# Wider joins, a moved chain of forget gates, a tile for the bonus factors and another estimate in a trunk layer

## The chip, the core and the metric

The kernel runs on one core of one Trainium2 chip. The metric is the device time of one launch in microseconds (us), as the median of several runs; lower is better. The core's engines are PE (TensorE: matmuls, with its weight loads shown as PEld), DVE (VectorE), ACT (ScalarE), POOL (GpSimd) and SP (SyncE, which here only starts DMAs). Each engine works off its own list of instructions in order and waits on semaphores for what the others make.

## The reference

One layer on 512 tokens and 16 meta tokens put ahead of them (T = 528), width 1024. A projection of the normed input feeds a recurrent branch (RWKV7, 8 heads of 64), an attention branch with forget gates (FoX, 8 heads of 64) and two gates; their outputs are projected, gated, added, projected again, and an MLP follows.

```python
u = rmsnorm(h, norm_mix); proj = u @ w_in
y_rw = rwkv7_branch(proj[..., :C_RW], ...)      # recurrence S = S(diag(w) + a^T b) + v^T k, y = S r
#   ... y = groupnorm(y);  bonus = sum(r * k * r_k) * v;  out = (y + bonus) * g
y_fx = fox_branch(proj[..., C_RW:C_RW + C_FX], ...)
#   ... log_f = log_sigmoid(fl + b_f);  F = cumsum(log_f);  logits = q.k * scale + F_q - F_k
gates = sigmoid(proj[..., C_RW + C_FX:] + b_gate)
h = h + (gates_A * (y_rw @ w_out_rw) + gates_B * (y_fx @ w_out_fx)) @ w_o
h = h + square(relu(rmsnorm(h) @ w_up)) @ w_down
```

## The kernel before

**The first half, the mixer.** Features stand on partitions, tokens along the free dimension. Each weight matrix comes in blocks of 128 output features. A block is loaded by SP (`wraw`), rounded by ACT into `whi` (L548), its rest taken by DVE as `wlo` (L549), and multiplied in three passes (`projections`, L579: `whi` by `uhi`, `whi` by `ulo`, `wlo` by `uhi`). There are 24 such blocks of features in two parts of 264 tokens (some with one part of 512), and 16 of gates with 512 tokens. Their rows are named `pj`. Around them run two branches:

- The recurrence works on pairs of heads, 128 partitions each, in groups of two pairs (`recurrent`). For a pair, `decay` makes the decays (a scan `lc`, L882), `keys` norms the keys (`sq`, `pkk`, L894 to L913), POOL makes one product of the keys (`BK`, L912), `rows` makes the left factors `L` (L919 to L923) and a POOL product `sq` for the bonus (L924), `scores` multiplies chunk by chunk (`psr`, L948, and transposes `pbt`, L955), and `bonus` multiplies by `rkb`, a block of ones scaled by the bonus factors (L928, `pbn` L931). `rkb` shares the buffer "yT" with the tile `yT` of the group norm (L1160 to L1163) and with `tmp` of the inverse.
- For each group `inverse` inverts 18 triangular 64x64 matrices: first the 16x16 blocks by a long chain on DVE (L985, L986, transposes, `Dn` at L997), then joins by small matmuls (`pw`): L1011 makes a product of 64 matmuls of 32x32, DVE masks it to `W2` (L1012), L1017 and L1020 (64 each) multiply `W2` with the inverses of the 32x32 blocks, in one column order and in the other. Then L1033 and L1040 (32 each) join 32x32 blocks to 64x64. `W2` is zero but for the lower left 16x16 of each 32x32 block, and of the first result (`p1`, added to `Dn`) only the blocks of the even quarters of the partitions are read behind it.
- `chain` then runs the recurrence over nine chunks (`pch`: L1093, L1099, L1121, each of which waits for the one before through a DVE copy), and `group_norm` closes it.
- The attention takes pairs of heads as well: `fox_features` norms queries and keys (`pssq`, L674) and transposes values; `attention` makes scores (`psc`, L740), softmax on DVE and ACT, transposes (`ppt`, L777) and the product with the values (`py`, L791, L794). It needs the running sum `F` of the log forget gates: `forget` (L620 to L630) makes it of a row tile `f0` of 8 partitions by two ACT and four DVE operations, a scan among them (L629), stores it to DRAM, and each pair loads it back, spread over the partitions (`nF`, L728).

**What sets the order.** The branches are streams (generators). `Turns.run` lets the stream of the best rank go on whose inputs are ready by an estimate (`Clock`): every instruction is booked with a cost from `RATE` (a fixed part and one per element), and PE's order in the first half is the order in which the streams issue. Where no branch is ready, `pj` matmuls are taken: they are the filling between dependent steps. PE's order is thus fixed when the program is built; DVE, ACT, POOL and SP are ordered by the scheduler of the framework, `after` adding a few edges. In `recurrent`, `forget()` is called behind the `scores` of the first pair.

**The second half** (from L1251 on) multiplies by the output weights, norms, and runs the MLP with a Strassen-like scheme; there the matmuls follow each other nearly without a gap.

Of the kernel before, what the change touches and what calls it, by code (L numbers as in the profile page):

```python
# [9 lines left out]
F32 = mybir.dt.float32  # L10
# [9 lines left out]
T = 528  # L20
# [18 lines left out]
C_RK = 30  # L39
# [23 lines left out]
class Clock:  # L63
# [35 lines left out]
    def read(self):  # L99
# [3 lines left out]
        for x in new:  # L103
# [28 lines left out]
            else:  # L132
                size = max([cols(a) for a in outs + (ins if "Reduce" in str(x.opcode) else [])])
                if eng in self.RATE and "DMA" not in str(x.opcode):
                    fixed, per = self.RATE[eng]
                    end = self.book(eng, max(deps, self.last(out)), fixed + per * size) + fixed + per * size
                else:
                    cost = 0.3 + size * 128 * 4 / 2.0e5
                    end = self.book("DMA", max(deps, self.last(out)), cost) + cost + 2.0
# [48 lines left out]
def kernel(ctx, tc, ht, x, win, par, cst, gain, lora, wout, wo, wup, wdn, out, dbg=None):  # L188
# [97 lines left out]
    with ExitStack() as st:  # L286
# [32 lines left out]
        llo = up.tile([128, 2, T], F32R, name="llo")  # L319
        fF = kp.tile([8, T], F32, name="fF", tag="Bm", bufs=2)  # L320
        fF_d = dr.tile([8, T], F32, name="fF_d")
        f0 = kp.tile([8, T], F32, name="f0", tag="L0", bufs=2)
        f1 = kp.tile([8, T], F32, name="f1", tag="L1", bufs=2)
        lfs = [rp.tile([128, TP], F32, name=f"lf{i}", tag=("okk", "orr")[i]) for i in range(2)]
# [294 lines left out]

        def forget():  # L620

            s_ = act(f0, f0, AF.Identity, bias=pr[:8, C_BF:C_BF + 1])
            V.scalar_tensor_tensor(f1, f0, -1.0, f0, ALU.mult, ALU.max)
            pin = pinned(s_)
            after(act(f1, f1, AF.Exp, scale=-1.0), pin)
            after(act(f1, f1, AF.Ln, bias=1.0), pin)
            V.scalar_tensor_tensor(f1, f0, 0.0, f1, ALU.min, ALU.subtract)
            V.memset(f0, 1.0)
            V.tensor_tensor_scan(fF, f0, f1, 0.0, ALU.mult, ALU.subtract)  # L629
            nc.sync.dma_start(fF_d, fF)  # L630
            forgot.done = True

        class Fox:
# [33 lines left out]
            def normed(self, d, parts, gcol):  # L667
# [9 lines left out]
                c0 = parts[0][0]  # L677
                act(sq[:, c0:], sq[:, c0:], AF.Exp, scale=-0.5)
                V.scalar_tensor_tensor(f, f, gcol, sq[:, c0:], ALU.mult, ALU.mult)
                return f  # L680

        def fox_features():
# [4 lines left out]
            for p, x in enumerate(fox):  # L687
# [7 lines left out]
                k = yield from x.normed(x.dk, x.WHOLE, pr[:, C_KG:C_KG + 1])  # L695
                x.k_done.done = True
                yield x.v_in
                yield lambda: max(ck.ready(x.v), banks(2))
# [145 lines left out]
        class Pair:  # L844
# [70 lines left out]
            def rows(self):  # L915
# [7 lines left out]
                A.copy(l1[hss[1], :, 64:], l0[hss[1], :, 64:])  # L923
                G.tensor_tensor(self.sq[:, :S], self.orr[:, 64:], self.sg[:, 64:], ALU.mult)  # L924

            def bonus(self):
                rkb = rp.tile([128, 128], F32, name="rkb", tag="yT")
                after(V.tensor_scalar(rkb, ones_blk, self.col(C_RK), None, ALU.mult), last["DVE"])  # L928
                yield lambda: max(ck.ready(rkb, self.sq), banks(1))
                bp = psm("pbn")  # L930
                mm(bp, rkb, self.sq[:, :S], start=True, stop=True)  # L931
                self.bv = bv = rp.tile([128, S], F32, name="bv", bufs=2)
                V.tensor_tensor(bv, bp, self.ov[:, 64:], ALU.mult)
                act(bv, bv, AF.Identity, bias=self.col(C_LB))
# [25 lines left out]
        def inverse(g, Bms, late):  # L960
# [54 lines left out]
            for n, pr_, c in cells:  # L1015
                for q in range(4):
                    mm(p1[qs[q], n, :], Tt[qs[q], c, pr_, half(q)], W2[qs[q], n, :], start=True, stop=True)  # L1017
            for n, pr_, c in cells:
# [152 lines left out]
        def recurrent():  # L1171
# [4 lines left out]
            for g in range(2):  # L1176
                prs = pairs[2 * g:2 * g + 2]
                for j, q in enumerate(prs):
# [12 lines left out]
                    if g == 0 and j == 0:  # L1191
                        forget()
                    if j == 0:
# [406 lines left out]
```

## Time and profile before

| what | value |
|---|---|
| median of 3 runs | 837.0 us (835.97 to 838.46) |
| the profiled execution | 836.0 us |
| its span, first to last instruction | 834.2 us |
| PE busy in the span | 810.9 us (97%), 6014 matmuls, as many weight loads |
| DVE, ACT, POOL busy | 605.0, 452.7, 123.1 us |
| DMA | 95.90 MB in 51484 packets |

The span is what the views of the profile cover; 1.8 us of the profiled time lie around it. Of an instruction a row gives the start and the duration in us, then the engine, line, operation, result and operands, sizes, and in brackets the idle time of the engine ahead of it and what ended that. Matmuls overlap, so the distance of two starts says more of the rate than a duration does. A matmul of plain fp32 stands twice in the trace, one of fp32r and a transpose once; each has a weight load of its own.

### The profile page before, as it was taken

What the parts mean: (1) busy time and instruction counts of PE and PEld (TensorE: products, weight loads), DVE (VectorE), ACT (ScalarE), POOL (GpSimd) and SP (SyncE); (2) the same over time, 40 slices, a digit from 0 to 9 for tenths busy, and PEclk for the clock granted to TensorE, in tenths of its full rate; (3) what the DMA queues carried; (4) which work ended last, traced back from release to release, by engine and by line L of the source; (5) the groups of instructions that cost most, each with busy time, mean ns of one, the idle gap of its engine ahead of it and who ended that gap; (6) DMA issues with size and microseconds to landing.
All of it is one profiled execution on the core that took longest, in us unless ns stands there. A gap on an engine that the chain in (4) does not pass through costs nothing.

```text
span 834.2 us, 15768 instructions
## 1 busy us (share of the span) xinstructions
PE 810.9 (97%) x6014; PEld 666.4 (80%) x6014; DVE 605.0 (73%) x1197; ACT 452.7 (54%) x941; POOL 123.1 (15%) x123
## 2 busy tenths in 40 slices
PE   8989989999999899999999999999999999999998
PEld 6979877777868777677878889888888888888886
DVE  6797975596878836676356744975698679867988
ACT  7767537766666347764456623665345434543452
POOL 1031000010001000000022002100650074007400
PEclk9999999999999989999999999999999999999999
DMA  7231221221121402123587603632743274336532
GB/s 239 69 100 55 74 70 55 65 83 59 51 90 52 128 28 79 43 85 102 171 274 223 214 14 122 182 102 59 244 155 98 90 226 153 87 113 203 157 109 75
DMA packets 51484, 95.90 MB, mean 115 GB/s; under 512 B 5832, under 2 KB 7240, under 8 KB 51408
## 3 DMA queue, kind: packets, MB, share of 16 engines
q1 hardware_dynamic: 47680, 86.37, 32.8%
q0 software_dynamic: 1280, 4.20, 1.7%
q10 hardware_dynamic: 2448, 4.33, 1.5%
q8 instruction: 47, 0.77, 0.4%
q14 instruction: 29, 0.24, 0.1%
HBM read 88.56 MB, written 6.31 MB: 114 GB/s over the span
## 4 chain that ended last, share of the span: by engine, by line
PE 85%; DVE 7%; ACT 3%; issue 2%; DMA 2%; SPq 0%; DVEq 0%; ACTq 0%
PE pj L579 22%; PE po L1341 21%; PE po L1468 12%; PE pd L1468 5%; PE po L1251 4%; PE po L1313 3%; PE pj L394 1%; PE pd L1282 1%; PE po L1282 1%; PE psc L740 1%; PE py L794 1%; PE psr L948 1%; PE pssq L674 1%; DVE wlo L549 1%; PE ppt L777 1%
## 5 line engine op out<-in xcount | busy, mean ns | idle before, releaser
L579 PE MATMUL pj<-uhi,whi 128*128 128x264 f32 (+1 forms) x480 | 166.8, 347 | 0.0
L579 PE MATMUL pj<-uhi,wlo 128*128 128x264 f32 (+1 forms) x480 | 154.5, 322 | 2.5 <-DVE wlo L549 2.5
L579 PE MATMUL pj<-ulo,whi 128*128 128x264 f32 (+1 forms) x480 | 154.5, 322 | 0.0
L240 DVE TENSOR_TENSOR wlo<-wraw,whi 128x512 fp32r<-128x512 f32 x84 | 82.5, 993 | 33.5 <-ACT whi L240 33.5
L579 PEld LDWEIGHTS pj<-uhi,whi 128*128 128x128 f32 x480 | 91.0, 190 | 13.7 <-issue 5.3
L579 PEld LDWEIGHTS pj<-uhi,wlo 128*128 128x128 f32 x480 | 90.9, 189 | 9.8 <-DVE wlo L549 2.9
L579 PEld LDWEIGHTS pj<-ulo,whi 128*128 128x128 f32 x480 | 91.2, 190 | 6.6 <-issue 1.9
L1341 PE MATMUL po<-zlo,whi 128*128 128x512 f32 (+1 forms) x248 | 94.8, 382 | 0.0
L1341 PE MATMUL po<-zhi,whi 128*128 128x512 f32 (+1 forms) x248 | 94.8, 382 | 0.0
L1341 PE MATMUL po<-zhi,wlo 128*128 128x512 f32 (+1 forms) x248 | 94.8, 382 | 0.0
L240 ACT CAST whi<-wraw 128x512 fp32r<-128x512 f32 x84 | 51.2, 616 | 51.4 <-PE po L1341 17.0
L548 ACT CAST whi<-wraw 128x512 fp32r<-128x512 f32 x78 | 47.8, 617 | 43.4 <-PE pj L579 40.7
L549 DVE TENSOR_TENSOR wlo<-wraw,whi 128x512 fp32r<-128x512 f32 x78 | 53.8, 695 | 17.6 <-ACT whi L548 17.2
L1390 POOL TENSOR_TENSOR t<-traw 128x512 f32<-128x512 f32 x24 | 38.6, 1626 | 173.1 <-DMA traw<-in_wdn 120.9
L274 ACT CAST whi<-t 128x512 fp32r<-128x512 f32 x64 | 39.9, 623 | 44.5 <-DVE wlo L274 27.2
L1468 PE MATMUL po<-wlo,fhi 128*128 128x512 f32 (+1 forms) x164 | 63.4, 387 | 0.1
L1468 PE MATMUL po<-whi,flo 128*128 128x512 f32 (+1 forms) x164 | 62.8, 384 | 0.0
L1468 PE MATMUL po<-whi,fhi 128*128 128x512 f32 (+1 forms) x164 | 62.3, 384 | 0.0
L274 DVE TENSOR_TENSOR wlo<-t,whi 128x512 fp32r<-128x512 f32 x64 | 43.5, 689 | 24.3 <-ACT whi L274 24.0
L1357 ACT CAST fhi<-R 128x768 fp32r<-128x768 f32 (+1 forms) x32 | 30.2, 944 | 48.3 <-DVE R L1364 24.9
L1341 PEld LDWEIGHTS po<-zhi,wlo 128*128 128x128 f32 x248 | 46.6, 188 | 9.1
L1341 PEld LDWEIGHTS po<-zlo,whi 128*128 128x128 f32 x248 | 46.6, 188 | 9.1
(330 smaller groups left out, 1701.8 us busy)
## 6 DMA issues: line engine op xcount, KB each, us to landing
wraw<-in_win SPq DMA_DIRECT2D x84, 256.0 KB, 2.6
wraw<-in_wup SPq DMA_DIRECT2D x60, 256.0 KB, 3.1
wraw<-in_wdn SPq DMA_DIRECT2D x48, 256.0 KB, 2.7
traw<-in_wdn SPq DMA_DIRECT2D x48, 256.0 KB, 3.5
gd<-gt ACTq DMA_DIRECT2D x16, 256.0 KB, 2.2
wraw<-in_wout SPq DMA_DIRECT2D x16, 256.0 KB, 3.8
gl<-gd SPq DMA_DIRECT2D x16, 256.0 KB, 3.5
traw<-in_wdn POOLq DMA_DIRECT2D x16, 256.0 KB, 3.1
```

What stands on the lines that cost most here:

```text
L240: casts.append((A.copy(hi, raw), low.tensor_tensor(lo, raw, hi.bitcast(F32), ALU.subtract)))
L274: return A.copy(hi, x), V.tensor_tensor(lo, x, hi.bitcast(F32), ALU.subtract)
L548: after(A.copy(hi, raw), last["ACT"])
L549: after(V.tensor_tensor(lo, raw, hi.bitcast(F32), ALU.subtract), last["DVE"])
L579: mm(po, a, b[:, k, a0:a1], start=n == 0, stop=n == 23)
L1251: mm(po, a, ys[k][:, b, :], start=n == 0, stop=n == 11)
L1282: mm(pd[i], a[:, k, 128 * i:128 * i + 128], b, start=k == 0 and n == 0, stop=k == 7 and n == 2)
L1313: mm(po, a[:, k, 128 * i:128 * i + 128], b[:, k, :], start=n == 0, stop=n == 23)
L1341: mm(po[:, t0:t1], a, b[:, k, t0:t1], start=n == 0, stop=n == 23)
L1357: A.copy(fhi[:, j, a:b], R[:, a:b])
L1390: eng.tensor_tensor(t, sums[c, pair] if c in (T1, T2) else c, d, ALU.add)
L1468: mm(x[i][:, cols], a[:, k, left, 128 * rows:128 * rows + 128], c[:, cols], start=start and k == 0 and n == 0, stop=stop and k == n_pairs ...
```

## The change

Four things are changed.

1. In `inverse`, the first product with `W2` is made by 32 matmuls with 32 rows and 64 columns (L1026) in place of 64 of 32x32: those of the odd quarters are left out, whose results nothing reads, and the weights of the even ones are as wide as both quarters.
2. `forget` is split. `biased` (the ACT operation that adds the bias) stands where `forget` stood; the rest is issued by `fox_features` behind the keys' norm of the first pair, in tiles of the attention's pool (the buffers of `nF0`, `nF1` and `pT0`), and the memset of ones goes from DVE to POOL. `normed` now keeps its last ACT operation as `d["s"]`.
3. `rkb` has a buffer of its own and is made in `rows`.
4. `Clock` counts the part per element of a DVE operation twice if it is a scan, if its result has an innermost stride over 4 elements, or if it transposes from such a stride.

```diff
+                    if eng == "DVE" and (getattr(x, "is_tensor_tensor_scan", False) or any(a.ap[-1][0] > 4 for a in outs + (ins[:1] if "Transpose" in str(x.opcode) else []))):
+                        per *= 2
...
-        fF = kp.tile([8, T], F32, name="fF", tag="Bm", bufs=2)
-        f1 = kp.tile([8, T], F32, name="f1", tag="L1", bufs=2)
...
-        def forget():
-
-            s_ = act(f0, f0, AF.Identity, bias=pr[:8, C_BF:C_BF + 1])
-            V.scalar_tensor_tensor(f1, f0, -1.0, f0, ALU.mult, ALU.max)
-            pin = pinned(s_)
-            after(act(f1, f1, AF.Exp, scale=-1.0), pin)
-            after(act(f1, f1, AF.Ln, bias=1.0), pin)
-            V.scalar_tensor_tensor(f1, f0, 0.0, f1, ALU.min, ALU.subtract)
-            V.memset(f0, 1.0)
-            V.tensor_tensor_scan(fF, f0, f1, 0.0, ALU.mult, ALU.subtract)
+        forgets = [fp.tile([8, T], F32, name=f"forget{i}", tag=tag) for i, tag in enumerate(("nF0", "nF1", "pT0"))]
+        def biased():
+            return act(forgets[0], f0, AF.Identity, bias=pr[:8, C_BF:C_BF + 1])
+        def forget(prev):
+            fa, fb, fF = forgets
+            V.scalar_tensor_tensor(fb, fa, -1.0, fa, ALU.mult, ALU.max)
+            pin = pinned(prev)
+            after(act(fb, fb, AF.Exp, scale=-1.0), pin)
+            after(act(fb, fb, AF.Ln, bias=1.0), pin)
+            V.scalar_tensor_tensor(fb, fa, 0.0, fb, ALU.min, ALU.subtract)
+            G.memset(fa, 1.0)
+            V.tensor_tensor_scan(fF, fa, fb, 0.0, ALU.mult, ALU.subtract)
             nc.sync.dma_start(fF_d, fF)
...
-                act(sq[:, c0:], sq[:, c0:], AF.Exp, scale=-0.5)
+                d["s"] = act(sq[:, c0:], sq[:, c0:], AF.Exp, scale=-0.5)
...
                 x.k_done.done = True
+                if p == 0:
+                    forget(x.dk["s"])
...
+                self.rkb = rp.tile([128, 128], F32, name="rkb")
+                after(V.tensor_scalar(self.rkb, ones_blk, self.col(C_RK), None, ALU.mult), last["DVE"])
             def bonus(self):
-                rkb = rp.tile([128, 128], F32, name="rkb", tag="yT")
-                after(V.tensor_scalar(rkb, ones_blk, self.col(C_RK), None, ALU.mult), last["DVE"])
+                rkb = self.rkb
...
             for n, pr_, c in cells:
-                for q in range(4):
-                    mm(p1[qs[q], n, :], Tt[qs[q], c, pr_, half(q)], W2[qs[q], n, :], start=True, stop=True)
+                for e, hs in enumerate(hss):
+                    mm(p1[hs, n, :], Tt[qs[2 * e], c, pr_, :], W2[qs[2 * e], n, :], start=True, stop=True)
...
                     if g == 0 and j == 0:
-                        forget()
+                        biased()
```

What the scheduler makes of it is seen in the engines' orders. The first place is PE's at the joins of the first group; the row of the scores `psc` and the `pj` rows are filling there. Before:

```order
L740 MATMUL psc<-ka,qa 128x144 x2
L674 MATMUL pssq<-fsq,cs 128x512
L579 MATMUL pj<-uhi,whi 128x512
L579 MATMUL pj<-ulo,whi 128x512
L579 MATMUL pj<-uhi,wlo 128x512
L1017 MATMUL pw<-AX_1271,Tt 32x32 x64
L1020 MATMUL pw<-Tt,AX_1271 32x32 x64
```

In the changed kernel (its lines are 9 further down):

```order
L748 MATMUL psc<-ka,qa 128x144 x2
L579 MATMUL pj<-uhi,whi 128x512
L579 MATMUL pj<-ulo,whi 128x512
L579 MATMUL pj<-uhi,wlo 128x512
L1026 MATMUL pw<-AX_1271,Tt 64x32 x32
L1029 MATMUL pw<-Tt,AX_1271 32x32 x64
```

The 128 matmuls in a row have become 96, and the norm's matmul `pssq` now stands behind them. Ahead of L1020 (the old L1011) there are six `pj` of 512 tokens more than there were.

The second place is DVE's order in the first pair of the recurrence, from the keys' factor `KT` to the first `wlo` behind the left factors `L`; `f` are the tiles of the forget gates, `lw` small weights. Before:

```order
L910 SCALAR_TENSOR_TENSOR KT<-okk,lc 128x9x64
L623 SCALAR_TENSOR_TENSOR f_112<-f_111 8x528
L911 SCALAR_TENSOR_TENSOR BK<-tha,KT 128x9x64
L308 SCALAR_TENSOR_TENSOR orr<-pj,pr_65,tm 128x264
L913 TENSOR_TENSOR KT<-BK,P 128x1152
L922 TENSOR_TENSOR L_661<-orr,P 128x9x64
L838 TENSOR_TENSOR lw_1920<-lraw,lw_1919 128x128
L627 SCALAR_TENSOR_TENSOR f_112<-f_111,f_112 8x528
L549 TENSOR_TENSOR wlo<-wraw,whi 128x512
```

Now:

```order
L918 SCALAR_TENSOR_TENSOR KT<-okk,lc 128x9x64
L310 SCALAR_TENSOR_TENSOR orr<-pj,pr_65,tm 128x264
L846 TENSOR_TENSOR lw_1903<-lraw,lw_1902 128x128
L919 SCALAR_TENSOR_TENSOR BK<-tha,KT 128x9x64
L310 SCALAR_TENSOR_TENSOR orr<-pj,pr_65,tm 128x264
L921 TENSOR_TENSOR KT<-BK,P 128x1152
L930 TENSOR_TENSOR L_662<-orr,P 128x9x64
L549 TENSOR_TENSOR wlo<-wraw,whi 128x512 x2
```

Both operations on `f` have left this stretch, and the one small weight `lw` behind `L` as well.

The third place is where they went: DVE's order at the keys of the second pair, from `sg` (the factor of the keys) to the normed keys `okk`. Before:

```order
L904 TENSOR_TENSOR sg<-sg,okk 128x528
L304 MEMSET tm 128x1
L308 SCALAR_TENSOR_TENSOR orr<-pj,pr_65,tm 128x264
L899 TENSOR_SCALAR sq<-pkk 128x264
L549 TENSOR_TENSOR wlo<-wraw,whi 128x512
L899 TENSOR_SCALAR sq<-pkk 128x264
L308 SCALAR_TENSOR_TENSOR orr<-pj,pr_65,tm 128x264
L905 SCALAR_TENSOR_TENSOR okk<-okk,pr,sq 128x528
```

Now (the row L635 is the scan):

```order
L912 TENSOR_TENSOR sg<-sg,okk 128x528
L306 MEMSET tm 128x1
L310 SCALAR_TENSOR_TENSOR orr<-pj,pr_65,tm 128x264
L633 SCALAR_TENSOR_TENSOR forget_432<-forget_431,forget_432 8x528
L549 TENSOR_TENSOR wlo<-wraw,whi 128x512
L635 SCALAR_TENSOR_TENSOR forget_433<-forget_431,forget_432 8x528
L907 TENSOR_SCALAR sq<-pkk 128x264 x2
L549 TENSOR_TENSOR wlo<-wraw,whi 128x512
L310 SCALAR_TENSOR_TENSOR orr<-pj,pr_65,tm 128x264
L913 SCALAR_TENSOR_TENSOR okk<-okk,pr,sq 128x528
```

And POOL's order at the same time, where the memset that the scan waits for stands behind the product `BK` of this pair:

```order
L826 MEMSET sg 128x48
L826 MEMSET orr 128x48
L920 TENSOR_TENSOR BK<-sg,lc 128x9x64
L634 MEMSET forget_431 8x528
L932 TENSOR_TENSOR sq<-orr,sg 128x512
```

One operation on the forget gates and the scan now stand ahead of the two `sq`, of which the first pair's place had two and the memset. Between `okk` and the product `KT` behind it, two `wlo` stood before; they now stand elsewhere, with one evacuation of the values (`ov`) in their place. PE takes six `pj` of 264 tokens more ahead of this pair's `pkk`.

## The prediction

> **What bounds the kernel now.** I read the busy time by halves first, then PE's waits in the half that the change touches, then PE's timeline at each wait. The windows view gives start and end of a stretch, its length, busy time and instructions of PE, PEld, DVE, ACT and POOL, the granted clock, the DMA share and GB/s.
>
> ```profile
> 0.00:421.50 421.50, 402.27 (x4122) 325.47 (x4122) 299.80 (x772) 256.18 (x609) 24.68 (x51) 0.99 0.27 87
> 421.50:834.20 412.70, 408.66 (x1892) 340.95 (x1892) 305.24 (x427) 196.56 (x333) 98.40 (x72) 1.00 0.46 143
> ```
>
> PE sets the end in both halves: it is idle for 19.2 us of the first and 4.0 of the second. The change leaves the second half as it is, and of PE's own work it alters only the joins. So its worth must come from PE's idle time in the first half, and from what PE does at less than its pace. The waits view, for PE in 0 to 422 us, gives who waited for whom, the sum, the number and the longest:
>
> ```profile
> PE pw L1020 <- issue: 5.8, 2, 3.5
> PE pj L579 <- DVE wlo L549: 2.5, 1, 2.5
> PE pbn L931 <- DVE rkb L928: 1.8, 1, 1.8
> PE pw L1011 <- DVE AX L997: 1.8, 2, 0.9
> PE pch L1099 <- DVE Rs L1095: 1.7, 3, 0.7
> ```
>
> The four largest stand at places that the change edits. The largest waits for no engine ("issue"), so I looked at PE's timeline around both of its stops:
>
> ```profile
> 116.89 0.40 PE L579 MATMUL pj<-uhi,wlo 128*128 128x512 f32 x1
> 117.22 1.26 PE L1017 MATMUL pw<-AX,Tt 32*32 32x32 f32 x126
> 118.33 1.07 PE L1020 MATMUL pw<-Tt,AX 32*32 32x32 f32 x102
> 121.72 0.46 PE L1020 MATMUL pw<-Tt,AX 32*32 32x32 f32 x24 [2.32 <-issue]
> 122.70 0.63 PE L579 MATMUL pj<-ulo,whi 128*128 128x512 f32 x1
> 123.12 0.63 PE L579 MATMUL pj<-uhi,wlo 128*128 128x512 f32 x1
> 125.75 0.39 PE L579 MATMUL pj<-uhi,whi 128*128 128x512 f32 x1
> 125.98 0.39 PE L579 MATMUL pj<-ulo,whi 128*128 128x512 f32 x1
> 126.53 1.20 PE L1033 MATMUL pw<-AX,Bm 32*32 32x32 f32 x64
> ...
> 288.79 1.26 PE L1017 MATMUL pw<-AX,Tt 32*32 32x32 f32 x126
> 289.90 0.45 PE L1020 MATMUL pw<-Tt,AX 32*32 32x32 f32 x31
> 293.88 1.50 PE L1020 MATMUL pw<-Tt,AX 32*32 32x32 f32 x95 [3.52 <-issue]
> ```
>
> Each stop lies inside a burst of 256 short matmul records, which with their weight loads are 512 entries of PE's queue in some 2.2 us (117.22, and the next row 1.11 later for the first half of them). The page and the DMA view of the two stops (windows 119 to 121.72 and 290.3 to 293.88) show what moves:
>
> ```profile
> q8 instruction: 47, 0.77, 0.4%
> ...
> q8 instruction: 1, 0.02, 2.9%
> ...
> q8 instruction: 1, 0.02, 1.5%
> ```
>
> Over the run, 47 packets of 16 KB for 6014 matmuls and as many weight loads make 256 entries each; in each stop exactly one packet moves. I read both as PE having run through its fetched instructions faster than they come. Counted on PE's order, a boundary of 256 entries falls where each stop begins, 24 of L1020's 128 records before its end in the first and 95 in the second (102 + 24 and 31 + 95 stand above; two more each are mixed with L1017's). The boundary before it lies 128 records earlier, in L1017: about 118.1 and 289.1. From there to the resumption at 121.72 and 293.88 it is 3.6 and 4.8 us: that is the supply for one block, against which a burst is to be measured.
>
> The Trainium skill ("Runtime: NRT & Kernel Launch", section "Instruction fetch mechanics") says that instructions come in blocks of 16 KiB, 256 each, and that the cost of crossing a boundary is mostly hidden. The packets agree with the size; the two stops of 2.32 and 3.52 us speak against hidden here, and were the page right for bursts too, the stops would have another cause and survive: that is rival A, below.
>
> **The change part by part.** The sum is made against the profiled execution (836.0 us), then moved by the 1.0 us by which the median (837.0) stands above it.
>
> *The stops (1).* Now 64 + 128 records of L1026 and L1029 take the place of 128 + 128, with psc and three pj ahead of them. In the new order a boundary falls 32 records into L1029 in both inverses, and the one before it near the end of the preceding L1020 (the old L1011). From there to the need lie some 0.2 us of that burst, psc, pj (in the first inverse 115.02 to 117.22 held psc, pssq and three pj, of which pssq's 0.56 leaves), L1026, and 0.3 of L1029: 3.7 to 3.9 us. Against a supply of 3.6 to 4.8 that leaves a wait of 0 to 1.1 in each. I take 0.4 each: 5.8 goes to 0.8, **-5.0** (-5.8 to -3.6).
>
> *The half clock behind the stops (2).* The granted clock after each:
>
> ```profile
> 121.90:125.30 3.40, 3.40 (x32) 2.66 (x21) 1.41 (x2) 0.00 (x0) 0.00 (x0) 0.50 0.02 5
> 292.60:299.40 6.80, 5.52 (x105) 3.81 (x105) 2.61 (x8) 0.32 (x1) 0.00 (x0) 0.50 0.01 2
> ```
>
> Behind both long stops it is 0.50, for 3.4 and 6.8 us, of which PE worked 3.4 and 5.5. At that clock two pj start 0.42 us apart (122.70, 123.12), at full clock 0.23 (125.75, 125.98): 45% of the time is lost. That is 1.5 us in the first. In the second PE resumes at 293.88: 5.5 us, 2.5. Of these 4.0 I keep 3.3 as gained, since pauses of up to a microsecond may still lower the clock for a slice at one place: **-3.3** (-4.0 to 0).
>
> *The tile for rkb (3).*
>
> ```profile
> 242.99 0.28 DVE L928 TENSOR_SCALAR rkb<-cs,pr 128x128 f32<-128x128 f32 x1
> 243.42 1.10 PE L931 MATMUL pbn<-sq,rkb 128*128 128x512 f32 x2 [1.84 <-DVE rkb L928]
> ```
>
> rkb waited for the group norm's yT, whose buffer it shared. With its own tile it is made with the left factors, long before. Four of its instructions move, one per pair, 0.28 us each, into `rows`, where DVE's other work surrounds them. Its other operand, POOL's sq, is made with the left factors as well. **-1.8** (-1.8 to 0, if something else is late there).
>
> *The first pair (4).* PE's longest wait for an engine is here:
>
> ```profile
> 46.30 0.69 DVE L623 SCALAR_TENSOR_TENSOR f<-f 8x528 f32<-8x528 f32 x1
> ...
> 49.92 0.27 DVE L838 TENSOR_TENSOR lw<-lraw,lw 128x128 fp32r<-128x128 f32 x1
> 50.12 0.69 DVE L627 SCALAR_TENSOR_TENSOR f<-f,f 8x528 f32<-8x528 f32 x1
> 50.74 0.67 DVE L549 TENSOR_TENSOR wlo<-wraw,whi 128x512 fp32r<-128x512 f32 x1
> ...
> 51.47 0.50 PE L579 MATMUL pj<-uhi,wlo 128*128 128x512 f32 x1 [2.49 <-DVE wlo L549]
> ```
>
> Two operations on f, 0.62 us each from start to next start, and lw (0.20) leave the stretch ahead of this wlo, while PE's order up to it stays. 1.4 of the 2.49 us go, 1.1 remain: **-1.4** (-2.5 to -0.5). The lower gain stands if the wlo is held by its operand instead.
>
> *The first joins (5).* L1011 waits for AX 0.86 and 0.93 us (1.8 in two). Ahead of it there are six pj of 512 tokens more in the first inverse, 1.4 us at 0.23, behind the same chain on DVE. In the second PE has more filling too, but the softmax of two blocks now stands in DVE's chain. **-1.6** (-1.8 to 0).
>
> *L1026 itself (6).* Half the records, twice the rows and columns. The nearest row is L1033 at 126.53: 64 records, two of the four rows of tiles in use, 1.20 us, as long as 128 records of L1017 with four. So no PE time is gained: **0** (-0.9 to +0.2 for both inverses; half of 1.1 us each would go if a record's count decided).
>
> *The change of tile size (7).* From the pj at 116.89 to the first 32x32 matmul it is 0.33 us, against 0.23 between pj: 0.1 for a change of tile. One more per inverse: **+0.2**. The Trainium skill ("TensorEngine Tiling (Array Packing)", section "Key Properties") says that changing the mode drains the engine, which speaks against a second tile shape in the joins; the 0.33 agrees in kind, and the sum would be the same by the row.
>
> *The second pair (8),* where the forget gates went.
>
> ```profile
> 74.64 1.42 POOL L912 TENSOR_TENSOR BK<-sg,lc 128x576 f32<-128x576 f32 x1 [20.71 <-DVE tm L304]
> ...
> 235.79 0.49 POOL L965 MEMSET Ain<- 128x448 f32 x1 [8.27 <-PE pyt L1152]
> ...
> 55.21 1.24 DVE L629 TENSOR_TENSOR_SCAN fF<-f,f 8x528 f32<-8x528 f32 x1
> ...
> 82.49 0.68 DVE L549 TENSOR_TENSOR wlo<-wraw,whi 128x512 fp32r<-128x512 f32 x1
> 83.77 0.68 DVE L549 TENSOR_TENSOR wlo<-wraw,whi 128x512 fp32r<-128x512 f32 x1
> ...
> 85.77 0.55 PE L955 MATMUL pbt<-cs,KT 128*128 128x128 f32 x3 [0.29 <-DVE KT L913]
> ```
>
> Here the scan (1.24) and one operation on f (0.62) stand ahead of both sq, and behind the scan's operation L633 the ones of POOL: its memset starts behind BK, at 76.1, and by the nearest memset takes 0.5, so the scan starts near 76.6 at the earliest. While it waits, DVE's two sq, orr and okk are queued behind it, and PE's psr and pbt wait for these. By this sq ends some 1.5 us later. Against it two wlo (1.2 us) leave the way to KT and one ov (0.45) enters, and PE has six pj of 264 more (6 x 0.12 = 0.7) ahead. Net +0.3 on the 0.29 that stands there: **+0.3** (-0.5 to +1.5; the upper end is the 1.5 with no filling). The forget DMA, the load of nF and the memset of POOL are over by about 86 us, and the first scores come at 115: no wait.
>
> *The rest (9).* Doubling some costs in the estimate reshuffles the recurrence's chain and the attention behind it; the order shows about as many dense steps of `pch` as before. pch waits 1.7 us in 3 of its 52 steps, 0.57 each. I take two more such waits, **+1.0** (-2.0, these and the 0.3 of pbt gone, to +4.0, seven more).
>
> Sum: -5.0 - 3.3 - 1.8 - 1.4 - 1.6 + 0 + 0.2 + 0.3 + 1.0 = -11.6, so 824.4 in the profiled execution's frame and **825.4** as median.
>
> **The rivals.**
>
> *A: the stops stay.* They have a cause that fewer records do not remove, or the boundary costs its 2.3 and 3.5 us wherever it falls in a burst; L1029 is still 128 records long. Against it: the page counts 47 packets, and only the two in the longest bursts stop PE. Terms 1 and 2 come back: 825.4 + 8.3 = 833.7.
>
> *B: the stops shorten, the clock still halves* behind one or both. For it: the clock is a reaction to idle time, and 0.4 to 1.1 us may remain. The price is 1.5 to 3.3: 827 to 829.
>
> *C: the change does not do what it says.* DVE is busy 71% of the first half, so waits removed at rkb, at the joins and in the first pair form again behind other operations (+4.8), on top of A: 838.5, no difference to be measured.
>
> *D: slower.* The order on PE is fixed by the estimate. If the doubled costs lead it to place the recurrence's steps with less filling than DVE needs, PE waits at `pch` step after step, 0.57 us each. It decides from (837.0 + 2.5 - 825.4) / 0.57 = 25 more of the 52 steps; 28 give 841. Against it: three of 52 wait now, and the new order is no denser.
>
> **How the numbers follow.** Forecast 0.57 at 825.4, its own range 819 to 830 (a part of the bounds of 1, 2, 4 and 9 at once; all at their ends would be 818 to 839). B 0.17, A 0.12, C 0.08, D 0.06. About 0.3% (2.5 us) is what a measurement of this kernel can tell from no change. Faster: forecast, B and two thirds of A, 0.82; same: C and a third of A, 0.12; slower: D, 0.06. The range 818 to 834 leaves out C, D and a part of A and of the forecast's tails, about 0.2.
>
> **What would show it.** In the changed kernel's waits of PE, "issue" at the joins' lines should be under 1.5 us in sum (A: near 5.8), and no slice of clock 0.50 should stand near 120 and 295 us (B: one or two). The wait of pbn for rkb should be gone, that of pj for wlo near 51 us be about 1.1, that of L1020 for AX near nothing. pbt or psr of the second pair should wait under 1 us, pch under 4. The forecast is wrong if the queue's boundary falls elsewhere than counted, or if DVE's new order in the second pair or in the chain makes PE wait by more than the bounds of 8 and 9.

## The result, and the profile after

| | time, us (median) | its profiled execution | span | ratio to before, with its 95% interval |
|---|---|---|---|---|
| before | 837.15 | 836.0 | 834.2 | |
| changed | 827.47 (826.25 to 829.23) | 826.42 | 824.6 | 0.9886 (0.9859 to 0.9912) |

The change gains 1.1%, 9.7 us in the medians and 9.6 in the spans; forecast were 11.6. Of all executions behind the tables and ratios here, one, of a kernel among the last experiments, took 1130.28 us at a mean granted clock of 0.655 and is left out. The windows view of the changed kernel, cut where the second half begins (columns as before: length, busy time of PE, PEld, DVE, ACT, POOL, clock, DMA share, GB/s):

```profile
0.00:412.00 412.00, 399.83 (x3995) 326.34 (x3995) 301.30 (x771) 255.21 (x609) 22.78 (x52) 1.00 0.28 89
412.00:824.60 412.60, 408.67 (x1892) 341.04 (x1892) 305.19 (x426) 197.51 (x333) 97.87 (x72) 1.00 0.46 144
```

The second half lasts 412.6 us against 412.7, so all of the gain lies in the first, 421.5 to 412.0. Its idle time on PE fell from 19.2 to 12.2. PE's waits there:

```profile
PE pj L579 <- DVE wlo L549: 2.5, 1, 2.5
PE pbt L964 <- DVE KT L921: 2.1, 2, 1.3
PE pch L1108 <- DVE Rs L1104: 1.7, 3, 1.2
PE warm L403 <- DVE ones L328: 1.5, 1, 1.5
PE psc L748 <- DVE nm L759: 1.5, 1, 1.5
```

The rows for issue (5.8), for rkb (1.8) and for AX ahead of the first joins (1.8) are gone. The wait for wlo stands at 2.5 as before, pbt waits 2.1 in place of 0.3, and psc has a wait of 1.5 that is new. PE's timeline at the first joins:

```profile
118.25 0.40 PE L579 MATMUL pj<-uhi,wlo 128*128 128x512 f32 x1
118.58 2.05 PE L1026 MATMUL pw<-AX,Tt 32*64 32x32 f32 x64
120.56 1.29 PE L1029 MATMUL pw<-Tt,AX 32*32 32x32 f32 x128
121.78 0.50 PE L579 MATMUL pj<-uhi,whi 128*128 128x512 f32 x1
```

No stop is left in either product. The 64 records of L1026 take 1.98 us (118.58 to 120.56), where the 128 of the old L1017 took 1.1.

### The profile page after: what moved, and what is told of

It is laid out like the page before. It is cut to its first block, busy times and chain, and to the rows that moved or that the text cites. A ratio compares the mean times of both kernels' runs of the same rounds, so it can differ in the third digit from the quotient of the medians.

```text
span 824.6 us, 15506 instructions
## 1 busy us (share of the span) xinstructions
PE 808.5 (98%) x5886; PEld 667.4 (81%) x5886; DVE 606.5 (74%) x1196; ACT 452.7 (55%) x941; POOL 120.6 (15%) x124
## 4 chain that ended last, share of the span: by engine, by line
PE 86%; DVE 5%; ACT 5%; issue 2%; DMA 1%; SPq 0%; POOL 0%; DVEq 0%; ACTq 0%
PE pj L579 22%; PE po L1350 21%; PE po L1477 12%; PE po L1260 5%; PE pd L1477 5%; PE po L1322 3%; PE pj L394 1%; PE po L1291 1%; PE pd L1291 1%; PE psc L748 1%; PE py L802 1%; PE psr L957 1%; PE ppt L785 1%; PE pch L1108 1%; DVE wlo L549 1%
## 5 line engine op out<-in xcount | busy, mean ns | idle before, releaser
L579 PE MATMUL pj<-uhi,whi 128*128 128x264 f32 (+1 forms) x480 | 164.2, 342 | 0.0
L242 DVE TENSOR_TENSOR wlo<-wraw,whi 128x512 fp32r<-128x512 f32 x84 | 80.3, 966 | 35.5 <-ACT whi L242 35.5
L549 DVE TENSOR_TENSOR wlo<-wraw,whi 128x512 fp32r<-128x512 f32 x78 | 52.7, 685 | 23.7 <-ACT whi L548 23.0
L1350 PEld LDWEIGHTS po<-zhi,whi 128*128 128x128 f32 x248 | 46.6, 188 | 9.0
```

The source lines that it names most:

```text
L242: casts.append((A.copy(hi, raw), low.tensor_tensor(lo, raw, hi.bitcast(F32), ALU.subtract)))
L549: after(V.tensor_tensor(lo, raw, hi.bitcast(F32), ALU.subtract), last["DVE"])
L579: mm(po, a, b[:, k, a0:a1], start=n == 0, stop=n == 23)
L1350: mm(po[:, t0:t1], a, b[:, k, t0:t1], start=n == 0, stop=n == 23)
```

## The experiments

**Where the gain lies, and whether the stops are PE's own instructions.** Four kernels, measured together. The first is the changed kernel with the old joins, the third the kernel before with the new ones:

```diff
-                for e, hs in enumerate(hss):
-                    mm(p1[hs, n, :], Tt[qs[2 * e], c, pr_, :], W2[qs[2 * e], n, :], start=True, stop=True)
+                for q in range(4):
+                    mm(p1[qs[q], n, :], Tt[qs[q], c, pr_, half(q)], W2[qs[q], n, :], start=True, stop=True)
```

> The changed kernel with the first product with W2 again as 64 matmuls of 32x32 (the other three parts stay). Theory (PE runs out of fetched instructions in a burst of 512 queue entries): a boundary of 256 entries falls 31 records before the end of the second product in the first inverse and 97 before it in the second, each with 128 quick records ahead of it. PE stops there for issue, 2 to 3.7 us each, the clock halves behind at least one of them; L1026 takes 1.1 us in place of 2.0. Time 827.5 + 5.8 + 3.5 - 1.8 = 835.0 (833.5 to 836.5). Rival (the stops had another cause, which the other three parts removed): no stop for issue, L1026 shorter by 0.9 each, 825.7.

Measured: 836.25 us, ratio 0.998 (0.9964 to 0.9997). Without the joins almost nothing of the gain is left. PE's timeline at the two inverses:

```profile
120.08 0.42 PE L1026 MATMUL pw<-AX,Tt 32*32 32x32 f32 x28 [0.78 <-issue]
...
120.35 1.02 PE L1029 MATMUL pw<-Tt,AX 32*32 32x32 f32 x96
123.81 0.65 PE L1029 MATMUL pw<-Tt,AX 32*32 32x32 f32 x31 [2.43 <-issue]
...
292.31 0.99 PE L1026 MATMUL pw<-AX,Tt 32*32 32x32 f32 x95 [0.76 <-issue]
...
296.04 1.27 PE L1029 MATMUL pw<-Tt,AX 32*32 32x32 f32 x97 [2.46 <-issue]
```

The stops are back, 31 and 97 records before the end, as counted. The burst is now stopped twice, at both boundaries in it, 128 records apart.

> The kernel before with the wide joins alone. Theory: both stops for issue go (-5.8), no half clock near 120 and 295 us (-4.0), L1026 costs 0.9 more in each inverse (+1.8), the waits at rkb (1.8) and at the first product for AX (1.8) stay: 837.1 - 8.0 = 829.1 (827.5 to 831). Rival (the gain needs the other parts as well): 833 or more.

The edit is the reverse of the diff above, in the kernel before. Measured: 827.63 us, ratio 0.9875 (0.985 to 0.99). Its waits of PE keep the two rows named in the expectation:

```profile
PE pj L579 <- DVE wlo L549: 2.5, 1, 2.5
PE pw L1011 <- DVE AX L997: 1.8, 2, 0.9
PE pbn L931 <- DVE rkb L928: 1.8, 1, 1.8
```

The forecast was 829.1, so the joins alone gained 1.5 us more than forecast, and they make the kernel as fast as the whole change. The other three parts remove 3.6 us of waits, at rkb and AX, and give most of it back elsewhere: the spans keep 0.9 of it (825.5 against 824.6), the medians 0.2.

> The kernel before with 32 more tiny matmuls (32x32) at the start, beside those that warm PE up: 128 entries more in PE's queue, nothing else is moved. Fetch theory: the stops move with the block boundaries, from 24 and 95 records before the end of the old L1020 to 88 and 31 records before it; their sum stays at 5 to 7 us. Rival (the stop belongs to the place in the program, to what the matmul reads or to another engine): the stops stay at 24 and 95 records before the end. Time 837 to 839 either way.

```diff
                     mm(warm[:, :128], ones, ones, start=True, stop=True)
+                for i in range(32):
+                    mm(warm[:32, :32], ones[:32, :32], ones[:32, :32], start=True, stop=True)
```

One execution, 838.91 us. PE's timeline, where L1022 is the old L1020:

```profile
121.38 0.54 PE L1022 MATMUL pw<-Tt,AX 32*32 32x32 f32 x38
123.91 0.94 PE L1022 MATMUL pw<-Tt,AX 32*32 32x32 f32 x88 [1.99 <-issue]
...
293.17 0.42 PE L1019 MATMUL pw<-AX,Tt 32*32 32x32 f32 x28 [0.59 <-issue]
...
293.43 1.03 PE L1022 MATMUL pw<-Tt,AX 32*32 32x32 f32 x96
297.17 0.65 PE L1022 MATMUL pw<-Tt,AX 32*32 32x32 f32 x31 [2.70 <-issue]
```

The stops moved from 24 and 95 to 88 and 31 records before the end, to the record. What was added lies a hundred us and more ahead of them. They belong to the block boundaries of PE's queue and not to a place in the program. In sum they are 5.3 us. The DMA records agree: a packet of q8, the queue of the instructions, ends 1.3, 1.5 and 1.5 us before PE resumes at 123.91, 293.17 and 297.17.

> The changed kernel with the first product with W2 made by 32 matmuls of 32x32 for the even quarters alone; the sum with Dn is then made for the even quarters alone by two DVE operations. As many queue entries as in the changed kernel, but weights of 32 columns. If the 64 columns are what costs (64 records in 1.98 us), L1026 falls to about 1.1 us, as L1033; if the two rows of tiles in use are, it stays at 2.0; if the count of records decides, 0.55. Fetch theory: the time from one boundary to the next falls from 4.7 to about 3.8 us, against a supply of 3.6 to 4.8, so a stop of 0 to 1 us may return in each inverse. Time 825.7 without stops, up to 829 with them and a half clock.

```diff
-                for e, hs in enumerate(hss):
-                    mm(p1[hs, n, :], Tt[qs[2 * e], c, pr_, :], W2[qs[2 * e], n, :], start=True, stop=True)
+                for q in (0, 2):
+                    mm(p1[qs[q], n, :], Tt[qs[q], c, pr_, :32], W2[qs[q], n, :], start=True, stop=True)
...
-            V.tensor_tensor(Dn, Dn, p1, ALU.add)
+            for q in (0, 2):
+                V.tensor_tensor(Dn[qs[q]], Dn[qs[q]], p1[qs[q]], ALU.add)
```

Measured: 828.49 us, ratio 0.9886 (0.9851 to 0.9922). The timeline:

```profile
120.04 1.16 PE L1026 MATMUL pw<-AX,Tt 32*32 32x32 f32 x61
...
121.07 0.45 PE L1029 MATMUL pw<-Tt,AX 32*32 32x32 f32 x31
122.08 1.01 PE L1029 MATMUL pw<-Tt,AX 32*32 32x32 f32 x95 [0.56 <-issue]
...
285.50 0.84 PE L1029 MATMUL pw<-Tt,AX 32*32 32x32 f32 x76 [1.66 <-issue]
```

L1026 falls to 1.0 us (120.04 to 121.03): the 64 columns of its weights are the cost, not the count of records. And with 1 us less between two boundaries the stops return, 2.2 us in sum, again where the boundaries were counted. What L1026 costs in the changed kernel is thus also what keeps the stops away, and only just: there the packet ahead of the boundary at 120.8 us ends at 119.3, and where PE stopped, it resumed 1.2 to 1.5 us after such an end.

**Does spreading the burst do as well?** The joins as they were, with the stream paused between the two products:

```diff
                     mm(p1[qs[q], n, :], Tt[qs[q], c, pr_, half(q)], W2[qs[q], n, :], start=True, stop=True)
+            if True:
+                t0 = ck.pe
+                yield lambda: t0 + 2.4
```

> The kernel before, joins as they were, with the stream of the recurrence made to pause between the first and the second product with W2, so that some ten pj of 512 tokens (2.2 us) stand between the two bursts; nothing else is edited. Fetch theory: what matters is how fast 256 entries run by, not the shape of the joins. From one boundary to the next it is now 3.2 us in the first inverse and 5.1 in the second, against supplies seen so far of 3.3 to 5.7: stops of 5.8 us fall to 0.1 to 2.5 in sum, the half clock goes or shrinks, 828 to 830. Rival (the wide joins gain by being wide, not by the time that they give): the stops stay near 5.8, 837.

Measured: 830.73 us, ratio 0.9913 (0.9887 to 0.9939). The first inverse runs through without a stop, in the second PE stops for 0.86, 0.80 and 1.81:

```profile
122.58 1.29 PE L1023 MATMUL pw<-Tt,AX 32*32 32x32 f32 x128
...
288.69 1.17 PE L1017 MATMUL pw<-AX,Tt 32*32 32x32 f32 x115 [0.86 <-issue]
...
292.42 0.44 PE L777 MATMUL ppt<-cs,pe 128*128 128x128 f32 x2 [0.80 <-issue]
...
295.88 0.31 PE L1023 MATMUL pw<-Tt,AX 32*32 32x32 f32 x2 [1.81 <-issue]
```

So seven tenths of what the wide joins alone gain (0.9875) come without any wide matmul. The time is just past the expected 830, and the stops are 3.5 us in sum where 0.1 to 2.5 were expected. The three lie at three boundaries in a row, 128 of PE's matmul records apart; the middle one falls in the filling between the joins, and PE stopped there too. From each to the next resumption it is 3.7 and 3.5 us, within the supply seen so far.

**The other three parts.** Three kernels, measured together: the changed kernel without the doubled costs; the changed kernel with the forget gates' chain at its old place; and the kernel before with the joins and the tile for rkb.

The first edit, against the changed kernel:

```diff
-                    if eng == "DVE" and (getattr(x, "is_tensor_tensor_scan", False) or any(a.ap[-1][0] > 4 for a in outs + (ins[:1] if "Transpose" in str(x.opcode) else []))):
-                        per *= 2
```

The second, against the changed kernel, with `forget` itself as it was before:

```diff
-                if p == 0:
-                    forget(x.dk["s"])
...
-                        biased()
+                        forget()
```

The third, against the kernel before, beside the diff of the joins:

```diff
+                self.rkb = rp.tile([128, 128], F32, name="rkb")
+                after(V.tensor_scalar(self.rkb, ones_blk, self.col(C_RK), None, ALU.mult), last["DVE"])
...
-                rkb = rp.tile([128, 128], F32, name="rkb", tag="yT")
-                after(V.tensor_scalar(rkb, ones_blk, self.col(C_RK), None, ALU.mult), last["DVE"])
+                rkb = self.rkb
```

> The changed kernel without the doubled costs in the estimate (joins, forget gates and the tile for rkb stay). The last run showed the joins alone as fast as the whole change, so some of the other parts must cost what they gain. Theory: the doubled costs cost it, by another order of PE: the wait of psc at 203 us (1.5) with the half clock behind it (about 1.5) and the second wait of pbt (0.8) go, the waits of the first product for AX (1.8) come back: 825.5 (824 to 827). Rival (the doubled costs pay for themselves by the 1.8 at AX, the forget gates cost): 829.

> The changed kernel with the forget gates' chain at its old place in the first pair of the recurrence, with the memset on DVE; PE's order is the same, row by row. Theory (the move frees 1.4 us of DVE in the first pair, which POOL's products take again, and costs a microsecond in the second pair): the wait for wlo near 52 us is 2.5 to 3.9, pbt in the second pair near 87 us waits under 0.5 in place of 0.8 and psr there 0.3 less; time 826.5 to 828. Rival (the move is worth its 1.4): wait for wlo 3.9, nothing gained in the second pair, 829.

> The kernel before with the wide joins and the tile for rkb alone. Theory: as the joins alone, less the wait of 1.8 at rkb: 825.8 (824.5 to 827), no wait of pbn. Rival (another operation is late there): 827.6. PE's order is that of the run without the doubled costs, so the two differ by the place of the forget gates alone.

| kernel | median, us | ratio to before | span of its profile, us |
|---|---|---|---|
| without the doubled costs | 827.91 | 0.989 (0.9873 to 0.9907) | 826.7 |
| forget gates at the old place | 826.71 | 0.9872 (0.9852 to 0.9892) | 823.4 |
| joins and rkb alone | 826.36 | 0.9871 (0.9853 to 0.9889) | 825.6 |

The intervals all overlap, so the times decide little; the profiles show where things stand. In two pairs of these kernels, counting the changed one, PE's order is the same row by row and only the forget gates differ: 824.6 against 823.4 with the doubled costs, 826.7 against 825.6 without. The move costs about 1.1 us of span in both. In the kernel with the old place the waits view has

```profile
PE pj L581 <- DVE wlo L551: 2.5, 1, 2.5
...
PE pbt L959 <- DVE KT L916: 1.3, 1, 1.3
```

where the changed kernel has 2.5 and 2.1: nothing is lost in the first pair, and the second pair's 0.8 goes. The doubled costs are worth 2.1 and 2.2 us of span by the two pairs of profiles (826.7 to 824.6, 825.6 to 823.4), but the medians give 0.4 for and 0.3 against. The medians mix executions of different granted clock. At a mean clock of 0.998 the four executions without the doubled costs took 827.88 to 828.54 us, and five of the changed order (two of the changed kernel, three of its repeat below) 825.91 to 826.74: 1.8 us on average, which sides with the profiles. The expectation that put a loss on the doubled costs missed: without them the wait of psc (1.5) goes, but 2.1 at AX and 1.0 at ppm stand in its place. The other two kernels came in their ranges. In the third the wait of pbn is gone; against the joins alone, waits of ppt (0.7), ppm (0.4) and AX (0.4 more) stand in its place.

**Who holds the wlo of the first pair?**

> The changed kernel with POOL's product sq of the first pair held until DVE has made the first Bm; the order of all engines is the same. Theory (DVE and POOL stand in each other's way: L930 took 1.82 us beside that product, 0.75 without one): L930 takes 0.75, the wait of pj for wlo near 52 us falls from 2.5 to 1.4, time 826.4. Rival (wlo is held by something else): the wait stays at 2.5.

```diff
-                G.tensor_tensor(self.sq[:, :S], self.orr[:, 64:], self.sg[:, 64:], ALU.mult)
+                self.gsq = lambda: G.tensor_tensor(self.sq[:, :S], self.orr[:, 64:], self.sg[:, 64:], ALU.mult)
+                if self.p:
+                    self.gsq()
...
-                    V.tensor_tensor(Bm[:, c0:c0 + 3, :], sb[:, :3, :], bc(tmask, 1, 3), ALU.mult)
+                    bm = V.tensor_tensor(Bm[:, c0:c0 + 3, :], sb[:, :3, :], bc(tmask, 1, 3), ALU.mult)
+                    if self.p == 0 and c0 == 0:
+                        after(self.gsq(), bm)
```

The edit changed no engine's order and the product started where it had, so this was a repeat of the changed kernel: 826.47 us, ratio 0.9883 (0.9853 to 0.9913), the wait 2.5. With a true dependency in place of the order:

```diff
-                        after(self.gsq(), bm)
+                        after(V.memset(self.sq[:, :1], 0.0), bm)
+                        self.gsq()
```

> The changed kernel with POOL's product sq of the first pair really held until the first Bm (by a DVE memset of one of its columns behind Bm, which the product overwrites; the edit of the run before this only ordered the program and did not hold it). Theory (DVE's L930 waits for the end of that product: 1.82 us beside it, 0.75 alone): L930 takes 0.75, the wait of pj for wlo near 52 us falls from 2.47 to about 1.4, time 826.4. Rival (wlo is held by something else): the wait stays at 2.47, 827.5.

First the changed kernel's timeline at this place, DVE, POOL and PE:

```profile
44.35 1.40 DVE L928 TENSOR_SCALAR L<-okk 128x9 f32<-128x9 f32 x1
...
49.36 1.82 DVE L930 TENSOR_TENSOR L<-orr,P 128x576 f32<-128x576 f32 x1
51.10 1.89 DVE L549 TENSOR_TENSOR wlo<-wraw,whi 128x512 fp32r<-128x512 f32 x3
...
43.92 1.80 POOL L920 TENSOR_TENSOR BK<-sg,lc 128x576 f32<-128x576 f32 x1 [8.01 <-ACT lc L893]
...
48.26 2.30 POOL L932 TENSOR_TENSOR sq<-orr,sg 128x512 f32<-128x512 f32 x1 [0.29 <-DVE orr L310]
...
51.84 0.50 PE L579 MATMUL pj<-uhi,wlo 128*128 128x512 f32 x1 [2.47 <-DVE wlo L549]
```

Then the kernel that holds the product:

```profile
49.11 0.75 DVE L930 TENSOR_TENSOR L<-orr,P 128x576 f32<-128x576 f32 x1
...
53.91 1.29 POOL L932 TENSOR_TENSOR sq<-orr,sg 128x512 f32<-128x512 f32 x1 [6.19 <-DVE sq L962]
...
50.52 0.50 PE L579 MATMUL pj<-uhi,wlo 128*128 128x512 f32 x1 [1.40 <-DVE wlo L549]
```

Time 826.42 us, ratio 0.9859 (0.9836 to 0.9882), an interval that overlaps the changed kernel's, so the rows show the effect and the time does not. The profiled execution took 823.37, the fastest of its four; no slice of half clock stands in it, which is worth another 1.5. L930 falls from 1.82 to 0.75 and PE's wait from 2.47 to 1.40, by the 1.07 that DVE no longer stands. In the changed kernel L930 ends 0.62 us after the product (48.26 + 2.30 = 50.56, 49.36 + 1.82 = 51.18), close to the 0.75 that it takes alone, so it did next to nothing until the product was over. L928, 9 elements wide, takes 1.40 beside BK and ends with it; in the kernel before, with BK already over, it took 0.16. In the kernel before it was POOL that stood:

```profile
48.14 5.53 POOL L924 TENSOR_TENSOR sq<-orr,sg 128x512 f32<-128x512 f32 x1 [0.29 <-DVE orr L308]
```

The Trainium skill ("SBUF — State Buffer", section "SBUF: two separate sides") says that DVE and POOL share a pair of ports as an exclusive lock, which a DVE operation takes if it has two inputs in SBUF, as L930 has, or runs in one of its two-port modes: whoever starts first has it for the whole instruction, and the other blocks fully. The rows agree, with 1.07 us on DVE in one kernel and some 4.2 on POOL in the other (5.53 against 1.29). Why DVE kept the lock through its row of operations before, and not after, no run here shows.

**Put together.** Two more kernels take up what the runs bore out. The first has the even quarters with a pause behind the first product, and the forget gates at the old place; the second has the even quarters, the same pause and POOL's product held. The pause stands between the two products in both, with the edit of the even quarters as above:

```diff
+            if True:
+                t0 = ck.pe
+                yield lambda: t0 + 1.2
```

> The changed kernel with the forget gates at their old place, the first product with W2 by 32 matmuls of 32x32 for the even quarters (1.0 us in place of 2.0, with the sum with Dn in two operations) and a pause of the recurrence's stream behind it, so that 5 to 12 pj stand between the two products. Theory: L1026 gives 1.0 us in each inverse, the pause keeps the time from boundary to boundary near 5 us so that no stop of over 0.5 returns, and the forget gates give 1: 827.5 - 2.0 - 1.0 = 824.5 (823 to 826). Rival (the time is only moved: what PE saves there it waits for DVE's longer chain at the next join): 826.7.

Measured: 826.38 us as the median of three executions, ratio 0.9869 (0.985 to 0.9889). The expectation missed, and the rival's 826.7 is what came: no stop is left and the first product takes 1.1 us, but waits of ppt (1.0 and 0.6) and po (1.1) are new. By ratio it is no faster than the kernel with the old forget gates alone (0.9872). Its span of 822.3 is 1.1 under that kernel's 823.4, but that profile holds a slice of 0.55 at 204 us, about 1.5 us, and this one holds none.

> The changed kernel with the two edits that the runs bear out: POOL's product of the first pair held until the first Bm, and the first product with W2 by 32 matmuls of 32x32 with a pause of the stream behind it. Theory: 1.1 at the wlo and 1.0 at each join, 827.5 - 3.1 = 824.4 (822.5 to 826); wait for wlo 1.4, no stop for issue. Rival (PE's order changes behind the pause, and waits of the recurrence or the attention take 1 or 2 us back, as in the run with the old forget gates): 826.

Measured: 823.61 us (822.81 to 824.71), ratio 0.9826 (0.9813 to 0.984). This beats the changed kernel's 0.9886, the intervals lie apart, and it is within the expectation. Its waits and its first join:

```profile
PE pbt L969 <- DVE KT L921: 2.1, 2, 1.3
...
PE pj L579 <- DVE wlo L549: 1.4, 1, 1.4
...
PE psc L748 <- DVE y_rw L1181: 0.9, 1, 0.9
```

```profile
117.52 1.20 PE L1031 MATMUL pw<-AX,Tt 32*32 32x32 f32 x64
...
120.39 1.29 PE L1037 MATMUL pw<-Tt,AX 32*32 32x32 f32 x128
```

The sum behind the expectation did not come as written. Neither this profile nor that of the held product alone has a slice of half clock, and their spans are 821.9 and 821.6: the shorter first product gains nothing there, and waits of ppt (1.0 and 0.6) are new again. What differs is the granted clock of all executions: 0.999 to 1.000 in the five of this kernel, 0.995 to 1.000 in the four of the held product alone, 0.995 to 0.999 in the three of the kernel ahead of this one. It is the only one of the three in which both PE's wait for wlo (1.4 for 2.5) and that of psc (0.9 for 1.5) are short. That the half clock stays away for this reason is likely, but was not tried.

## Why the prediction was right in the whole, and where it was not

Sign and range were right; the forecast gain of 11.6 us was too large by 1.9. The mechanism was right for the joins. For the rest two of the three waits went as forecast, but nearly as much formed again elsewhere. The joins' terms (1, 2, 6 and 7) were put at -8.1 in sum, and the joins alone gave 8.7 in the spans and 10.5 in the medians. The other terms were put at -3.5, and the other three parts gave 0.9 in the spans and next to nothing in the medians. Term by term, in the profiled executions:

- **The stops (1)**, -5.0 forecast, -5.8 measured. The cause is shown by the shifted queue. The size was short because L1026 takes 2.0 us and not the 1.2 of its nearest row: from boundary to need it is 4.7 us and not 3.7 to 3.9, and the 0.4 us that I left in each inverse did not come. The kernel of even quarters, with 1 us less, shows those remains (0.56 and 1.66). That the full 5.8 went is therefore luck in part: it hangs on the cost that term 6 missed.
- **The half clock (2)**, -3.3 forecast. At the joins all 4.0 went. It is no trait of one profile: the mean granted clock is 0.989 to 0.994 in the 36 executions of the kernel before that were measured with the experiments, and 0.995 to 1.000 in the four of the joins alone. But the new wait of psc was followed by one in the changed kernel's profile:

```profile
202.85 1.23 PE L748 MATMUL psc<-ka,qa 64*128 64x256 f32 x4 [1.52 <-DVE nm L759]
```

```profile
204.00:207.40 3.40, 3.40 (x27) 3.15 (x27) 3.19 (x9) 1.97 (x4) 0.28 (x2) 0.52 0.00 1
```

  At 45% of 3.4 us that gives 1.5 back.
- **rkb (3)** and **the first joins (5)**: -1.8 each was measured, -1.8 and -1.6 forecast. Both waits are gone.
- **The first pair (4)**, -1.4 forecast, nothing measured (2.49 and 2.47). This step failed. Both operations on f and lw had left the stretch as the order said, but the step priced DVE's operations by their rows of before, and POOL's products, which had stood aside there, now took the time from L928 and L930. Held back, the product gives 1.07 of it.
- **L1026 (6)**, 0 forecast with +0.2 as the bound, +0.9 in each inverse measured, +1.8. The step failed in its nearest row: L1033 has two rows of tiles in use, as L1026, but weights of 32 columns. The prediction's "twice the rows and columns" is wrong too: the row says 32*64, so only the columns doubled. The bound on the upper side was taken from nothing that had 64. The Trainium skill ("TensorE: Matmul & The Clock Gate", section "LDWEIGHTS (loading the stationary operand)") says that a weight load's time goes by its columns; the even quarters agree in kind, 1.0 against 2.0 us.
- **The change of tile size (7)**, +0.2 forecast. It was not measured apart: the 0.33 us from the pj at 118.25 to L1026 stood there before, and the change that is new, from L1026 to L1029, lies within the 1.98 us of (6).
- **The second pair (8)**, +0.3 forecast, up to +1.5 as bound, about +1.1 of span measured by the pairs of kernels that differ in the forget gates alone. The size was off: the second operation on f, too, stood beside POOL's product and took 1.60 us where 0.69 was counted. pbt waits 0.8 there in place of 0.3, psr 0.7 in place of 0.2.

```profile
75.18 1.60 DVE L633 SCALAR_TENSOR_TENSOR forget<-forget,forget 8x528 f32<-8x528 f32 x1
...
74.81 1.41 POOL L920 TENSOR_TENSOR BK<-sg,lc 128x576 f32<-128x576 f32 x1 [23.44 <-DVE tm L306]
```

- **The rest (9)**, +1.0 forecast for two more waits of pch. pch waits 1.7 as before; the cost came elsewhere, 1.5 at psc, which waits for the softmax, and 1.3 at the third pair's pbt. Against it two waits of the kernel before went, so that +1.1 remain:

```profile
PE ppm L775 <- ACT pm L760: 1.0, 1, 1.0
...
PE po L1251 <- DVE gl L1253: 0.7, 1, 0.7
```

So measured, the terms add up to -5.8 - 4.0 + 1.5 - 1.8 - 1.8 + 0 + 1.8 + 1.1 + 1.1 = -7.9, of a difference of 9.6. The other 1.7 us were not traced to a place.

Of the rivals A is excluded (no stop is left at the joins), B holds at neither join, and C holds in the main for three parts of the four: most of what the tile for rkb and the estimate removed formed again elsewhere, and the forget gates' move removed nothing, so that with the old joins 0.2% of gain is left. D is excluded: pch waits in 3 steps, 1.7 us in sum, as before.

## What to carry to other kernels

In this kernel a burst of small matmuls was limited by how fast PE's instructions came, and not only by its own time. Count the queue entries: a matmul and its weight load, twice for plain fp32. Every stop came where 256 of them had run by in 1.3 to 4.0 us since the boundary before, and none where they took longer; some stretches of 3.4 to 3.9 us also passed without one (before the change, that of 3.4 up to 289.07 us). So put other work between such bursts, or use fewer and slower matmuls. A shorter burst gives its time only if PE does not wait for it elsewhere: the weights of half the columns with a pause saved 1.7 us in the products and nothing in the span.

An operation that leaves DVE frees its time only if nothing else there then stands beside a POOL product; look for rows longer than their fellows of the same shape. And compare executions at the same granted clock, or a difference of 1.5 us can be one slice of half clock.

## What the runs showed of the hardware

- **Supply of instructions.** From a block boundary to the resumption behind the next it took 3.3 to 4.8 us in thirteen of fourteen stops (before, old joins, even quarters, shifted, spread) and 5.7 us in one, the even quarters' second. Each time the trace has one 16 KB packet of q8 between the two: it starts 1.0 to 2.5 us after the boundary and takes 0.9 to 1.5 us, and PE resumes 1.2 to 1.5 us after its end. In the stop of 5.7 the packet took 2.6 us, beside the highest DMA share of these stretches (0.71); that the other transfers slowed it was not tried.
- **The half clock does not follow from the length of a stop alone.** psc's wait of 1.52 us at 203 us was followed by a slice of 0.52 in the changed kernel, the same wait of 1.5 by none with POOL's product held. The wait of 2.5 at the first wlo was followed by none before and after, but by slices of 0.7 to 0.8 in five other runs. Each pair of such slices, like the one of 0.52, costs about 1.5 us, so single profiles differ by that; what decides was not tried.
